# Position bias rows from a repeated table in memory, and another room for a low part

## The chip, the cores and the metric

The kernel runs on one core of one Trainium2 chip. TensorE (PE) multiplies matrices into PSUM; VectorE (DVE), ScalarE (ACT) and GpSimd (POOL) work on SBUF and PSUM; SyncE (SP) issues almost all transfers between the chip's memory (DRAM) and SBUF, which 16 DMA engines carry. The metric is the device time of one execution, in microseconds.

## The reference

One layer over 512 tokens of width 2048, in float32. Two mixers run in parallel on projections of the normalised input: a gated linear recurrence in 8 heads, and an attention of 8 heads in which an indexer picks 128 keys for each query and a position bias from a table of 32 buckets is added to the scores. Both are gated, projected, merged, projected out and normalised. What the change touches are the bias and the end of the recurrence:

```python
bias = jnp.moveaxis(bias_table[t5_bucket(top_idx - t_pos[None, :, None])], -1, 2)
logits = jnp.where(valid[:, :, None, :], logits + bias, -jnp.inf)
...
o = rmsnorm(o, gnorm_w).reshape(b_, s_, A_WIDTH)
return (o * jax.nn.silu(a_g.astype(F32))).astype(a_q.dtype)
```

The bias depends on key position minus query position alone. Over a block of 128 queries and the 256 keys that end with it, row p of the bias is the same row of 384 values, read from 127 - p on.

## The kernel before

Every float32 product is made of three products of a high and a low part (`split`, `mm3`): ScalarE rounds a tile to the high part, VectorE subtracts it for the low part. Weights come in blocks of 512 KB. `load` issues a block into one of two raw buffers (`wr`); a block is split when TensorE begins the block two ahead of it (`prep`, or `high_parts` with its `low_parts` one step later), and a raw buffer is free for the next load when the low part is made. `load_ahead` issues loads as buffers come free.

The order is written out by hand. `jobs` is a list of matmul jobs; each calls `pump()` every few matmuls. `pump()` issues free loads, calls `flush()` (which issues stores put off by two pumps, kept in `late`), and takes one step of each of six generators, its lanes: `hgrn`, `top`, `att`, `norm`, `misc`, `t5`. Every engine executes its own instructions in the order in which the program gives them; SP too has one such order.

`t5_gen` makes the bias. It multiplies the bias table by a one-hot matrix of buckets (two matmuls into 8 x 384), subtracts each head's first value, splits the result and stores both parts in memory (`t5_d`). Then, for two heads at a time, it loads 128 overlapping rows of 256 values with a step of one value between partitions (`bf`, a load for each part), multiplies both by a flipped identity (`flip`) so that the row order is reversed, copies the product out of PSUM and stores 128 x 256 values for each head in `bh_d`. Each pair of heads takes four steps of the lane. Before the attention, `att_bias(h)` loads `bh_d[h]`, and GpSimd adds it to the mask.

`hgrn_gen(p)` runs the recurrence for two heads at once (pairs 3, 2, 0, 1 in this order). It ends with `o` (in the room of `hf`), its squares (`hk`), their sums over a head (`hz`, matmuls with ones), and the gated output `hy`, of which high and low parts of two heads are stored in `ya_d` by four put-off stores. The rooms of these four parts are `hkd`, `hst`, `hq` and `hS`. For pairs 3, 2 and 0 the rooms of `hf`, `hk` and `hq` lie in the pool `norms`, which is given back before the attention; pair 0 uses those of pair 3. `hS` and `hkd` are one room for all pairs: the next pair's `hks` copy (L859) goes into the same one.

`ai_job(3)`, `ai_job(2)` and `af_aq(0)` are the matmul jobs that run while `t5_gen` and the first two recurrences do.

Of the kernel before, what the change touches and what calls it, by code (L numbers as in the profile page):

```python
# [44 lines left out]
F32 = mybir.dt.float32  # L45
FR = mybir.dt.float32r
AF = mybir.ActivationFunctionType
OP = mybir.AluOpType
# [4 lines left out]
T, D = 512, 2048  # L53
NK = D // 128
H, HD = 8, 128
# [13 lines left out]
def hybrid_block(ctx, tc, x, norm_w, w_in, lb_table, gnorm_a, q_norm_w, kv_norm_w, w_uq,  # L69
# [3 lines left out]
    V, A, G, PE, SP = nc.vector, nc.scalar, nc.gpsimd, nc.tensor, nc.sync  # L73
# [9 lines left out]
    dram = ctx.enter_context(tc.tile_pool(name="scratch", bufs=1, space=DRAM))  # L83
    ctx.enter_context(tc.manual_schedule())

    def bank(name):
        return sdp.tile([128, 512], F32, name=name, tag="sd")

    def split(hi, lo, src):
        A.activation(hi, src, AF.Copy)  # L90
        V.tensor_tensor(lo, src, hi.bitcast(F32), op=OP.subtract)  # L91
# [6 lines left out]
    def mm(ps, l, r, first, last):  # L98
        PE.matmul(ps, l, r, start=first, stop=last, skip_group_check=True)  # L99
# [13 lines left out]

    ya_d = dram.tile([2, H, 128, T], F32, name="ya_d")
    yb_d = dram.tile([2, H, 128, T], F32, name="yb_d")
    t5_d = dram.tile([2, H, 384], F32, name="t5_d")
    gate_d = dram.tile([48, 128, T], F32, name="gate_d")
    bh_d = dram.tile([H, 128, 256], F32, name="bh_d")
    m21_d = dram.tile([2, 128, 8, 256], F32, name="m21_d")
    ckv_d = dram.tile([2, 128, T], F32, name="ckv_d")  # L120
    cq_d = dram.tile([4, 128, T], F32, name="cq_d")
# [13 lines left out]
    R = SimpleNamespace(load=0.0)  # L135
# [82 lines left out]
    late = [[], []]  # L218
# [266 lines left out]
    def t5_gen():  # L485
        rb = R.i.tile([128, H], F32, name="rb")
        rbs = [R.i.tile([128, H], FR, name=f"rb{i}") for i in "hl"]
        oh = R.i.tile([128, 384], FR, name="oh")
        tl = R.i.tile([H, 384], F32, name="tl")
        ts = [R.i.tile([H, 384], FR, name=f"tl{i}", tag=f"sum{i}") for i in "hl"]  # L490
        flip = R.i.tile([128, 128], FR, name="flip")
        far = R.i.tile([H, 1], F32, name="far")
        G.memset(rb, 0.0)
        SP.dma_start(rb[0:32], rel_bias)
        raw = R.i.tile([128, 512], F32, name="nt", bufs=2)
        SP.dma_start(raw[:, 0:384], c_buckets)
        SP.dma_start(raw[:, 384:], c_flip)
        yield
        yield
        A.activation(oh, raw[:, 0:384], AF.Copy)  # L500
        A.activation(flip, raw[:, 384:], AF.Copy)
        split(*rbs, rb)
        yield
        ps = bank("t5")
        for i, r in enumerate(rbs):
            mm(ps[:H, :384], r, oh, i == 0, i == 1)
        V.tensor_copy(far, ps[:H, 0:1])
        V.tensor_scalar(tl, ps[:H, :384], far, None, op0=OP.subtract)
        A.activation(ts[0], tl, AF.Copy)
        yield  # L510
        V.tensor_tensor(ts[1], tl, ts[0].bitcast(F32), op=OP.subtract)
        for i in range(2):
            late[1].append(lambda i=i: SP.dma_start(t5_d[i], ts[i].bitcast(F32)))
        for _ in range(3):
            yield
        for h in range(0, H, 2):
            bf = R.i.tile([128, 2, 2, 256], FR, name="bf")
            for i in range(2):
                SP.dma_start(bf[:, i].bitcast(F32), bass.AP(tensor=t5_d.tensor, offset=t5_d.offset + (i * H + h) * 384,
                                                            ap=[[1, 128], [384, 2], [1, 256]]))  # L520
            for _ in range(3):
                yield
            ps = bank("t5")
            for i in range(2):
                mm(ps, flip, bf[:, i].rearrange("p h c -> p (h c)"), i == 0, i == 1)
            e = R.i.tile([128, 2, 256], F32, name="nt", bufs=2)
            V.tensor_copy(e, ps.rearrange("p (h c) -> p h c", h=2))
            late[1].append(lambda h=h, e=e: SP.dma_start(bh_d[h:h + 2].rearrange("h p c -> p h c"), e))
            yield

    def lb_gen():
# [182 lines left out]
    def place(p, shape, dtype, name, tag):  # L714
        if p == 1 or tag not in ("hf", "hk", "hq"):
            return R.h.tile(shape, dtype, name=name, tag=tag)
        return R.i.tile(shape, dtype, name=name, tag=f"{tag}{p or 3}")
# [60 lines left out]
    def aq_evac(p):  # L778
        def evac(c, ps):
            if c == 0:  # L780
                hg[p, "q"] = place(p, [128, 2, T], F32, "hq", "hq")
            q = hg[p, "q"][:, c, :]
            A.activation(q, ps, AF.Sigmoid)
            V.scalar_tensor_tensor(q, ps, 128 ** -0.5, q, op0=OP.mult, op1=OP.mult)
            if c == 1:
                lanes["hgrn"].append(hgrn_gen(p))
        return evac

    def hgrn_gen(p):
        f, k, q = (hg[p, n] for n in "fkq")  # L790
# [78 lines left out]
        for l in range(8):  # L869
# [10 lines left out]
            ps = bank("hl")  # L880
# [76 lines left out]
        for c in range(2):  # L957
            ps = bank("hz")
# [10 lines left out]
        yield  # L969
        R.load = 2.4  # L970
        for c in range(2):
            y = [place(p, [128, T], FR, f"hy{i}", (("hkd", "hst"), ("hq", "hS"))[i][c]) for i in range(2)]
            split(*y, sq[:, c])
            for i in range(2):
                late[1].append(lambda y=y[i], i=i, h=2 * p + c: SP.dma_start(ya_d[i, h], y.bitcast(F32)))
# [46 lines left out]

    def att_bias(h):
        bh = R.a.tile([128, 256], F32, name="bh")
        SP.dma_start(bh, bh_d[h])
        at_[h, "g"] = R.a.tile([128, T], F32, name="ag", bufs=2)
        SP.dma_start(at_[h, "g"], gate_d[8 + h])
        MB = R.a.tile([128, 4, 256], F32, name="MB")

        def add(b):  # L1030
            if b:
                e = MO[b] + (b + 1) * 128
                G.tensor_tensor(MB[:, b, :], R.M[:, e - 256:e], bh, op=OP.add)
            else:
                G.tensor_tensor(MB[:, 0, 128:], R.M[:, 0:128], bh[:, 128:], op=OP.add)

        return MB, add
# [71 lines left out]
    def att_gen(p):  # L1109
        def rest(n):  # L1110
            for _ in range(n + (p > 0)):
                yield

        while lanes["top"]:
            yield
        MB, add = att_bias(2 * p)
        for two in ((3, 2), (0, 1)):
            for b in two:
                add(b)
            yield  # L1120
        P = yield from att_scores(p, 0, MB)
        MB, add = att_bias(2 * p + 1)
        for two in ((3, 2), (0, 1)):
            for b in two:
                add(b)
            yield
        yield from rest(1)
        PT = att_turn(P)
        yield from rest(2)
        att_values(p, 0, PT)  # L1130
        P = yield from att_scores(p, 1, MB)
        yield from rest(3)
        PT = att_turn(P)
        yield from rest(2)
        att_values(p, 1, PT)
        yield
# [174 lines left out]
    def end_index():  # L1311
        lanes["misc"].extend(waiting)
        drain("misc")
        leave("idx")
        leave("raws")
        R.h = enter("hgrn", side="right")
        lanes["hgrn"].extend((hgrn_gen(3), hgrn_gen(2)))
        lanes["norm"].append(norm_gen(R.ckv, 2, c_kvw, R.ckh, R.ckl))
        lanes["t5"].append(t5_gen())
# [355 lines left out]
```

## Time and profile before

| what | us |
|---|---|
| median of three runs | 1349.22 (1348.98 to 1350.01) |
| the profiled execution's own time | 1349.49 |
| its span in the trace | 1347.7 |
| TensorE busy | 1336.3 |
| VectorE busy | 1073.1 |
| ScalarE busy | 686.8 |
| GpSimd busy | 26.5 |

In rows of the profile, L12 is line 12 of the kernel; `out<-in` are the tiles or tensors that an instruction writes and reads, with numbers left out of their names (`t<-bf,flip` is the bias product in the bank `t5`, `t_d` is `t5_d`). A row of the timeline starts with the start and the duration in us; in square brackets stands the idle time of the engine ahead of it and what ended it. SPq is SP issuing a transfer: the duration there is that of the issue, and several of a line are taken together. In a list of waits the numbers are total us, times, longest us. In the rows of transfers they are the count, the size of one and the median us from issue to landing. The granted clock of TensorE was 0.999.

### The profile page before, as it was taken

What the parts mean: (1) busy time and instruction counts of PE and PEld (TensorE: products, weight loads), DVE (VectorE), ACT (ScalarE), POOL (GpSimd) and SP (SyncE); (2) the same over time, 40 slices, a digit from 0 to 9 for tenths busy, and PEclk for the clock granted to TensorE, in tenths of its full rate; (3) what the DMA queues carried; (4) which work ended last, traced back from release to release, by engine and by line L of the source; (5) the groups of instructions that cost most, each with busy time, mean ns of one, the idle gap of its engine ahead of it and who ended that gap; (6) DMA issues with size and microseconds to landing.
All of it is one profiled execution on the core that took longest, in us unless ns stands there. A gap on an engine that the chain in (4) does not pass through costs nothing.

```text
span 1347.7 us, 26963 instructions
## 1 busy us (share of the span) xinstructions
PE 1336.3 (99%) x11018; PEld 1244.6 (92%) x11018; DVE 1073.1 (80%) x1750; ACT 686.8 (51%) x1108; POOL 26.5 (2%) x47
## 2 busy tenths in 40 slices
PE   9999999999999999999999999999999999999997
PEld 8888999999999999999999898888888888899996
DVE  7978889988798888886778877975656658899856
ACT  8555444545554444445765655656443433444444
POOL 0000000000000000000000000020101100000000
PEclk9999999999999999999999999999999999999999
DMA  6245345544444445446224533445855556653563
GB/s 226 71 120 153 95 142 171 157 141 143 140 145 120 128 141 157 142 141 208 71 79 132 169 99 91 125 135 182 279 182 185 185 183 211 211 157 119 170 228 141
DMA packets 145310, 204.80 MB, mean 152 GB/s; under 512 B 10601, under 2 KB 87074, under 8 KB 145058
## 3 DMA queue, kind: packets, MB, share of 16 engines
q1 hardware_dynamic: 144898, 202.82, 48.2%
q8 instruction: 86, 1.41, 0.4%
q14 instruction: 38, 0.31, 0.1%
q10 hardware_dynamic: 288, 0.26, 0.1%
HBM read 167.89 MB, written 35.15 MB: 151 GB/s over the span
## 4 chain that ended last, share of the span: by engine, by line
PE 97%; DMA 1%; ACT 1%; DVE 1%; issue 0%; SPq 0%; DVEq 0%; ACTq 0%
PE pp L94 15%; PE pp L96 15%; PE pp L95 15%; PE acc L94 14%; PE acc L96 14%; PE acc L95 14%; PE acc L99 2%; PE hl L99 1%; PE ho L99 1%; PE sc L94 1%; PE sc L95 1%; PE sc L96 1%; DMA ya_d<-hy 0%; DMA x<-in_x_dram 0%; PE hp L99 0%; PE pt L378 0%
## 5 line engine op out<-in xcount | busy, mean ns | idle before, releaser
L169 ACT ACTIVATE bh<-wr 128x768 fp32r<-128x768 f32 x128 | 108.2, 845 | 211.8 <-issue 88.7
L171 ACT ACTIVATE wh<-sv 128x512 fp32r<-128x512 f32 x256 | 152.8, 624 | 88.3 <-DVE sv L164 69.9
L94 PE MATMUL pp<-s,wh 128*128 128x256 f32 x624 | 172.3, 276 | 0.0
L95 PE MATMUL pp<-s,wh 128*128 128x256 f32 x624 | 172.3, 276 | 0.0
L96 PE MATMUL pp<-s,wl 128*128 128x256 f32 x624 | 172.3, 276 | 0.0
L173 DVE TENSOR_TENSOR wl<-sv,wh 128x1024 fp32r<-128x1024 f32 x128 | 156.5, 1222 | 5.8
L172 DVE TENSOR_TENSOR bl<-wr,bh 128x768 fp32r<-128x768 f32 x128 | 122.3, 955 | 40.4 <-ACT bh L169 40.3
L94 PE MATMUL acc<-xh,wh 128*128 128x512 f32 x304 | 120.9, 398 | 0.0
L91 DVE TENSOR_TENSOR wl<-wr,wh 128x1024 fp32r<-128x1024 f32 (+1 forms) x74 | 88.9, 1201 | 39.4 <-ACT wh L90 39.2
L96 PE MATMUL acc<-xh,wl 128*128 128x512 f32 x304 | 118.7, 390 | 0.0
L95 PE MATMUL acc<-xl,wh 128*128 128x512 f32 x304 | 118.4, 390 | 0.0
L95 PEld LDWEIGHTS pp<-s,wh 128*128 128x128 f32 x624 | 117.2, 188 | 0.0
L96 PEld LDWEIGHTS pp<-s,wl 128*128 128x128 f32 x624 | 117.1, 188 | 0.0
L94 PEld LDWEIGHTS pp<-s,wh 128*128 128x128 f32 x624 | 117.1, 188 | 0.0
L94 PE MATMUL pp<-xh,bh 128*128 128x256 f32 x416 | 114.9, 276 | 0.0
L96 PE MATMUL pp<-xh,bl 128*128 128x256 f32 x416 | 114.9, 276 | 0.0
L95 PE MATMUL pp<-xl,bh 128*128 128x256 f32 x416 | 114.9, 276 | 0.0
L90 ACT ACTIVATE wh<-wr 128x1024 fp32r<-128x1024 f32 (+1 forms) x74 | 76.6, 1035 | 70.4 <-PE acc L95 37.7
L94 PE MATMUL acc<-yh,wh 128*128 128x512 f32 x256 | 100.2, 391 | 0.0
L96 PE MATMUL acc<-yh,wl 128*128 128x512 f32 x256 | 99.8, 390 | 0.0
L95 PE MATMUL acc<-yl,wh 128*128 128x512 f32 x256 | 99.7, 390 | 0.0
L164 DVE TENSOR_TENSOR sv<-wr 128x512 f32<-128x512 f32 x128 | 87.9, 687 | 11.7 <-DMA wr<-in_w_in_dram 8.8
(406 smaller groups left out, 3724.2 us busy)
## 6 DMA issues: line engine op xcount, KB each, us to landing
wr<-in_w_in_dram SPq DMA_DIRECT2D x136, 512.0 KB, 3.8
wr<-in_w_out_dram SPq DMA_DIRECT2D x32, 512.0 KB, 3.7
mg<-gate_d SPq DMA_DIRECT2D x48, 256.0 KB, 3.4
gate_d<-c SPq DMA_DIRECT2D x44, 256.0 KB, 5.3
wr<-in_w_in_dram SPq DMA_DIRECT2D x36, 256.0 KB, 3.1
wr<-in_w_pa_dram SPq DMA_DIRECT2D x16, 512.0 KB, 4.2
wr<-in_w_pb_dram SPq DMA_DIRECT2D x16, 512.0 KB, 4.4
wr<-in_w_qidx_dram SPq DMA_DIRECT2D x8, 512.0 KB, 4.4
```

Of the source, the lines that this page charges most:

```text
L90: A.activation(hi, src, AF.Copy)
L91: V.tensor_tensor(lo, src, hi.bitcast(F32), op=OP.subtract)
L94: PE.matmul(ps, lh, rh, start=first, stop=False, skip_group_check=True)
L95: PE.matmul(ps, lh, rl, start=False, stop=False, skip_group_check=True)
L96: PE.matmul(ps, ll, rh, start=False, stop=last, skip_group_check=True)
L99: PE.matmul(ps, l, r, start=first, stop=last, skip_group_check=True)
L164: V.tensor_tensor(sv[:, 0:2, :], b[:, 1:3, :], b[:, 0:1, :].to_broadcast([128, 2, 256]), op=OP.add)
L169: A.activation(bh, b[:, 1:4, :], AF.Copy)
L171: A.activation(vh[:, i:i + 2, :], sv[:, i:i + 2, :], AF.Copy)
L172: V.tensor_tensor(bl, b[:, 1:4, :], bh.bitcast(F32), op=OP.subtract)
L173: V.tensor_tensor(vl, sv, vh.bitcast(F32), op=OP.subtract)
```

## The change

The table `tl` (8 heads x 384 values, float32) is stored once, unsplit, in `t5_d`. For two heads at a time a transfer within memory copies each head's row 128 times into `bh_d`, which is now 128 x 384 for each head; the four transfers are issued in four steps of the lane in a row. `att_bias` reads row p of head h from element 127 - p on, by a step of 383 elements between partitions. The matmuls with `flip`, the split of the table, the loads of `bf` and the copies out of PSUM are gone. Apart from that, the low part of the second head of `hy` takes the room of `hf` in place of that of `hS`.

```diff
-    t5_d = dram.tile([2, H, 384], F32, name="t5_d")
+    t5_d = dram.tile([H, 384], F32, name="t5_d")
-    bh_d = dram.tile([H, 128, 256], F32, name="bh_d")
+    bh_d = dram.tile([H, 128, 384], F32, name="bh_d")
...
-        ts = [R.i.tile([H, 384], FR, name=f"tl{i}", tag=f"sum{i}") for i in "hl"]
-        flip = R.i.tile([128, 128], FR, name="flip")
...
-        raw = R.i.tile([128, 512], F32, name="nt", bufs=2)
-        SP.dma_start(raw[:, 0:384], c_buckets)
-        SP.dma_start(raw[:, 384:], c_flip)
+        raw = R.i.tile([128, 384], F32, name="nt", bufs=2)
+        SP.dma_start(raw, c_buckets)
...
-        A.activation(ts[0], tl, AF.Copy)
-        yield
-        V.tensor_tensor(ts[1], tl, ts[0].bitcast(F32), op=OP.subtract)
-        for i in range(2):
-            late[1].append(lambda i=i: SP.dma_start(t5_d[i], ts[i].bitcast(F32)))
-        for _ in range(3):
+        late[1].append(lambda: SP.dma_start(t5_d, tl))
+        for _ in range(4):
             yield
         for h in range(0, H, 2):
-            bf = R.i.tile([128, 2, 2, 256], FR, name="bf")
-            for i in range(2):
-                SP.dma_start(bf[:, i].bitcast(F32), bass.AP(tensor=t5_d.tensor, offset=t5_d.offset + (i * H + h) * 384,
-                                                            ap=[[1, 128], [384, 2], [1, 256]]))
-            for _ in range(3):
-                yield
-            ps = bank("t5")
-            for i in range(2):
-                mm(ps, flip, bf[:, i].rearrange("p h c -> p (h c)"), i == 0, i == 1)
-            e = R.i.tile([128, 2, 256], F32, name="nt", bufs=2)
-            V.tensor_copy(e, ps.rearrange("p (h c) -> p h c", h=2))
-            late[1].append(lambda h=h, e=e: SP.dma_start(bh_d[h:h + 2].rearrange("h p c -> p h c"), e))
+            SP.dma_start(bh_d[h:h + 2], bass.AP(tensor=t5_d.tensor, offset=t5_d.offset + h * 384,
+                                                ap=[[384, 2], [0, 128], [1, 384]]))
             yield
...
-            y = [place(p, [128, T], FR, f"hy{i}", (("hkd", "hst"), ("hq", "hS"))[i][c]) for i in range(2)]
+            y = [place(p, [128, T], FR, f"hy{i}", (("hkd", "hst"), ("hq", "hf"))[i][c]) for i in range(2)]
...
-        SP.dma_start(bh, bh_d[h])
+        SP.dma_start(bh, bass.AP(tensor=bh_d.tensor, offset=bh_d.offset + h * 128 * 384 + 127,
+                                 ap=[[383, 128], [1, 256]]))
```

More of the change, by code (lines that the diff above doesn't have):

```diff
@@ L494, in t5_gen @@
         SP.dma_start(rb[0:32], rel_bias)
-        raw = R.i.tile([128, 512], F32, name="nt", bufs=2)
-        SP.dma_start(raw[:, 0:384], c_buckets)
-        SP.dma_start(raw[:, 384:], c_flip)
+        raw = R.i.tile([128, 384], F32, name="nt", bufs=2)
+        SP.dma_start(raw, c_buckets)
         yield
         yield
-        A.activation(oh, raw[:, 0:384], AF.Copy)
-        A.activation(flip, raw[:, 384:], AF.Copy)
+        A.activation(oh, raw, AF.Copy)
         split(*rbs, rb)
```

## The prediction

> **What bounds the kernel now.** I read the page first, then who waited for whom on TensorE, then the chain, and then the DMA queue and ScalarE in order of time around the work that the change touches.
>
> ```profile
> PE 1336.3 (99%) x11018; PEld 1244.6 (92%) x11018; DVE 1073.1 (80%) x1750; ACT 686.8 (51%) x1108; POOL 26.5 (2%) x47
> PE 97%; DMA 1%; ACT 1%; DVE 1%; issue 0%; SPq 0%; DVEq 0%; ACTq 0%
> PE acc L335 <- POOL ones_r L305: 1.4, 1, 1.4
> ...
> PE hl L99 <- ACT hks L859: 0.4, 1, 0.4
> PE acc L95 <- issue: 0.3, 1, 0.3
> ```
>
> TensorE is busy for 1336.3 us of a span of 1347.7, and 97% of the chain is its own. Its waits are five rows (the first and the last two are shown) of 3.5 us in all. So time is won here only by taking instructions off TensorE, or those 0.4 us, and anything that makes TensorE wait is paid in full.
>
> **The removed work.** The flipped products are eight matmuls in four pairs; the first and the last of the four on the chain are these.
>
> ```profile
> 713.43 0.47 PE t L99 x2
> ...
> 754.67 0.47 PE t L99 x2
> ```
>
> Four pairs at 0.47 make 1.9 us. What goes with them (four copies out of PSUM and a subtraction on VectorE, two casts on ScalarE) lies beside a busy TensorE, since no row of its waits names them: nothing. If that cover were gone, it would still be a gain.
>
> **The other room.** The low part of the second head now lies where that pair's `o` was, and not in `hS`. What waited for `hS` stands on the chain.
>
> ```profile
> 802.52 6.12 DMA ya_d<-hy
> 808.72 1.07 ACT hks L859
> ```
>
> ScalarE's copy at 808.72 waited for a store of pair 2, and TensorE waited 0.4 us behind it: -0.4. The new room has later users too: pair 3's becomes pair 0's `hf`, and the rooms of pairs 2 and 0 become the attention's tiles. The nearest is pair 0's, at the last stores before the attention's `aq`:
>
> ```profile
> 858.55 2.35 SPq L975 DMA_DIRECT2D ya_d<-hy  x4
> ...
> 869.35 0.60 ACT L987 ACTIVATE aq<-acc 128x512 fp32r<-128x512 f32 x1 [0.91 <-PE acc L96]
> ```
>
> The last is issued by 860.9 and such a store lands in 4.8 (row below), at 865.7, ahead of 869.35: nothing. Uncovered, it would cost at most those 4.8 us.
>
> **The loads of the bias.** Eight loads of 128 rows of 1 KB stay eight, at addresses shifted by a row.
>
> ```profile
> ya_d<-hy SPq DMA_DIRECT2D x16, 256.0 KB, 4.8
> bf<-t_d SPq DMA_DIRECT2D x8, 256.0 KB, 4.3
> bh_d<-nt SPq DMA_DIRECT2D x4, 256.0 KB, 5.0
> bh<-bh_d SPq DMA_DIRECT2D x8, 128.0 KB, 4.1
> ```
>
> Their landing is bounded by 4.1 and, doubled, 8.2 us. Behind a load queue GpSimd's additions and VectorE's maxima; none of TensorE's five waits names these. Nothing, with at most 4 us at the first head if the cover fails.
>
> **The copies in memory.** This part decides. Eight loads of `bf` and four stores go; four copies come, memory to memory, each of 2 heads x 128 rows x 384 elements, 1,536 B to a row and 393,216 B to a copy. SP does not wait for TensorE, so where they come to stand is read from its queue.
>
> ```profile
> 696.57 0.40 SPq L513 DMA_DIRECT2D t_d<-tlh  x1
> 697.02 0.30 SPq L513 DMA_DIRECT2D t_d<-tll  x1
> 702.94 0.40 SPq L147 DMA_DIRECT2D wr<-in_w_in_dram  x1
> 703.43 0.97 SPq L519 DMA_DIRECT2D bf<-t_d  x2
> 708.75 0.37 SPq L147 DMA_DIRECT2D wr<-in_w_in_dram  x1
> 709.17 0.50 SPq L919 DMA_DIRECT2D hg<-gate_d  x1
> 718.15 0.37 SPq L147 DMA_DIRECT2D wr<-in_w_in_dram  x1
> ```
>
> The generator takes seven steps to the first transfer before and after, so copy 1 stands at 703.4. Before, the next pair came four steps later; now the copies stand in four steps in a row. Between two weight loads lie two steps, and a copy waits for nothing: copies 1 and 2 are issued at about 703.5 and 704, ahead of the weight load of 708.75 (call it W2), copies 3 and 4 at about 709.7 and 710.2, ahead of that of 718.15 (W3).
>
> What a copy costs behind it hangs on how many DMA engines carry it. The stretch from 696.3 to 702.9 (40 slices of 0.165 us), in which the two small stores follow a weight load, shows this:
>
> ```profile
> GB/s 0 0 0 0 0 68 124 87 137 106 180 304 366 391 391 379 379 236 146 34 0 0 99 0 0 0 0 0 0 0 0 0 0 0 0 0 0 0 0 0
> DMA packets 561, 0.57 MB, mean 86 GB/s; under 512 B 32, under 2 KB 560, under 8 KB 560
> ...
> wr<-in_w_in_dram SPq DMA_DIRECT2D x1, 512.0 KB
> t_d<-tlh SPq DMA_DIRECT2D x1, 12.0 KB
> t_d<-tll SPq DMA_DIRECT2D x1, 12.0 KB
> ```
>
> 561 packets are 512 rows of weights, 16 rows of 1,536 B, one instruction fetch, and 32 tiny ones. A transfer that counts 128 partitions first and two that count 8 rows first would leave 16 + 8 + 8 = 32 completions: I read these as one for each engine used, and the engines as dealt along the outermost count. The copies count 2 heads outermost. So they would run on two of the 16 engines, each with one head: 196,608 B. The trace holds no transfer of size with a short outermost count, so this price is bounded. Below: all 16 engines at 385 GB/s (the mean of the load's four best slices above) carry 393,216 B in 1.0 us, which delays nothing. Above: two engines at the mean of the stretch around it,
>
> ```profile
> q1 hardware_dynamic: 13363, 14.09, 40.9%
> ```
>
> 14.09 MB in 40.9% of 16 engines over 120 us (660 to 780): 17.9 GB/s for an engine, 11.0 us a copy. At the best slices' 24.1 GB/s for an engine it is 8.2 us. I take two engines, by the completions, and 8.2, since rows of 1.5 KB stand nearer to the best slices' rows of 1 KB than to a mean with single words in it.
>
> The Trainium skill ("DMA: Bandwidth & Descriptors", "Why a DMA increments its semaphore by 16 and not by 1") says that a transfer uses the largest number of engines up to 16 that divides the outermost counts of both its sides. The trace agrees as far as the 16 + 8 + 8 go. With that page's 27 GiB/s for an engine a copy would take 6.8 us (an estimate), and the sum below would be 5.6 us lower.
>
> The queue is one, so the weights' share on those two engines stands behind the copies. A load occupies the engines until about 3.3 us after its issue (traffic above ends in slice 20, at 699.6; it was issued some 0.3 ahead of the 696.57), 1.4 of them at full rate. From the load of 702.94: free at 706.2; copies 1 and 2 to 722.6; W2 to 724.0; `hg` to 725.4; copies 3 and 4 to 741.8; W3 to 743.2, landed by 743.6. Here is who wants them:
>
> ```profile
> 719.21 1.06 ACT L208 ACTIVATE wh<-wr 128x1024 fp32r<-128x1024 f32 x1
> ...
> 725.27 1.06 ACT L208 ACTIVATE wh<-wr 128x1024 fp32r<-128x1024 f32 x1 [0.99 <-PE acc L96]
> 726.36 1.28 ACT L961 ACT_TABLE_LOAD   x1
> 728.46 1.27 ACT L961 ACTIVATE hk<-hz,cols 128x512 f32<-128x512 f32 x2 [0.82 <-PE hz L99]
> 729.75 1.28 ACT L962 ACT_TABLE_LOAD   x1
> 731.04 1.06 ACT L962 ACTIVATE hk<-hk 128x1024 f32<-128x1024 f32 x1
> 732.00 1.07 ACT L743 ACTIVATE hv<-acc 128x512 f32<-128x512 f32 x2
> 732.96 1.06 ACT L208 ACTIVATE wh<-wr 128x1024 fp32r<-128x1024 f32 x1
> ...
> 736.22 0.63 ACT L90 ACTIVATE hy<-hk 128x512 fp32r<-128x512 f32 x1 [0.69 <-DVE hk L968]
> ```
>
> ```profile
> 737.96 0.39 PE L96 MATMUL acc<-xh,wl 128*128 128x512 f32 x1
> ...
> 745.34 0.40 PE L96 MATMUL acc<-xh,wl 128*128 128x512 f32 x1
> ```
>
> ```profile
> 732.19 1.22 DVE L211 TENSOR_TENSOR wl<-wr,wh 128x1024 fp32r<-128x1024 f32 x1
> ```
>
> With two raw buffers, W2 is split at 719.21 and W3 at 725.27; weights are split two blocks ahead, and W3's block starts with the third matmul, its first use of a low part, at 737.96. Now W2 makes ScalarE wait 5 us from 719.21; what that costs TensorE is swallowed by the next. W3 lands at 743.6: split to 744.7, low part to 745.9 instead of 737.96: 7.9 us of TensorE. Behind the waiting split stand ScalarE's table loads, logarithms, exponentials and copies of `hv` (1.28 + 1.27 + 1.28 + 1.06 + 1.07, to 750.7), the next split (751.7), two `hy` (753.0), and VectorE's last `hy` and low part (0.7 + 1.2: 754.9). That low part is the one of the next block, used at 745.34: the shift is now 9.6. The pairs of products ahead of it are within the stall and give nothing; the last pair and the room give 0.47 + 0.4 behind it. **The sum: +8.7 us.** On the profiled execution's 1349.49 that is 1358.2; it was 0.27 above the median of 1349.22, so I predict **1357.9** for the median. At 11.0 us a copy W3 lands 11.2 later: 1369.1. Below, 16 engines: -1.9 - 0.4, 1346.9.
>
> **The rivals.** No change here means within 0.2%, 2.7 us, about what a measurement of this kernel can tell.
> 1. *The rows, and not the heads, are dealt to the engines.* A copy is then 256 rows over 16 engines, 1.0 us, and the slack of W3 (landed at 718.15 + 3.8, split at 725.27) takes four of them: 1346.9, not slower. It decides from about 2 us a copy down. For it: all loads of size in the trace fill 16 engines. Against: 32 completions and not 48. Chance 0.20.
> 2. *The cover holds.* If copies 3 and 4 come to stand behind W3, it lands by 726, and only the load after it is late, at 743.6 against a split at 732.96; the two blocks ahead then absorb all but some 2.5 us, which the removed products pay: 1349.5. Against: nothing keeps SP from issuing them earlier. Chance 0.08.
> 3. *A row from memory to memory takes twice as long* (a read and a write at the same memory): 16.4 us a copy, 32.8 later, 1390.7. The stores' 4.8 us against the loads' 4.3 for the same 256 KB speak against double. Chance 0.05.
> 4. *Copies on 16 engines, and the freed engines or the moved tiles give more than the products.* TensorE's other waits are 3.5 - 0.4 us, so at most 3.1 more: 1343.8. They lie elsewhere in the code, which speaks against it. Chance 0.05.
>
> **How the numbers follow.** The forecast, a stall at W3, has 0.62. Slower: 0.62 + 0.05 = 0.67. Within 0.2%: the second rival's 0.08 and 0.13 of the first's, whose 2.3 us lie just inside: 0.21. Faster: the rest of the first, 0.07, and the fourth: 0.12. The forecast's own range is 1355 to 1369: its low end is the sum without the catch-up after W3 (7.9, less the two pairs behind it and the 0.4: +6.6), its high end 11.0 us a copy; with the first rival taken in it is 1346.4 to 1369, which leaves out the third, the fourth and the tails.
>
> **What would show it.** Right: the copies issued on SP at about 703.5, 704, 709.7 and 710.2, landing after 10 us and more, later ones later; a wait of ScalarE's split for weights of some 5 us near 719 and 15 or more near 726; a hole in TensorE near 738; no product on `flip`; no wait of `hks` for `ya_d`. The prediction is wrong if the copies land in about 5 us, if the weight loads behind them keep 3.8, or if the hole is elsewhere.

## The result and the profile after

The changed kernel takes 1360.37 us (median; 1359.5 to 1361.63) against 1349.28 beside it: a ratio of 1.0082, 95% interval 1.0069 to 1.0095. It is 11.1 us slower; 8.7 were forecast. The profiled execution's span grew from 1347.7 to 1359.8 us, by 12.1. That execution took 1361.63 us, 1.3 above the median of its kernel, so a sum read from its trace comes out about 1 us above the 11.1.

From the page of the changed kernel, engines and chain:

```profile
PE 1339.5 (99%) x11010; PEld 1245.6 (92%) x11010; DVE 1070.5 (79%) x1745; ACT 686.5 (50%) x1106; POOL 27.4 (2%) x47
...
PE 92%; DMA 3%; DVE 2%; ACT 1%; issue 1%; SPq 0%; DVEq 0%; ACTq 0%
```

TensorE has eight products less, and yet 3.2 us more busy time; its share of the chain fell from 97% to 92%. Who waited for whom on TensorE says where the rest went (total us, times, longest us):

```profile
PE acc L94 <- ACT wh L208: 4.7, 1, 4.7
PE hl L99 <- DVE hqs L809: 3.2, 1, 3.2
...
PE hz L99 <- DVE hzl L91: 1.2, 1, 1.2
```

Three new holes, 9.1 us. The wait of `hl` for `hks` behind the store is gone. On SP, the queue of transfers in order of time (start and duration in us):

```profile
703.25 0.37 SPq L147 DMA_DIRECT2D wr<-in_w_in_dram  x1
703.67 3.91 SPq L509 DMA_DIRECT2D bh_d<-t_d  x2
709.06 6.26 SPq L147 DMA_DIRECT2D wr<-in_w_in_dram  x1
715.37 1.91 SPq L901 DMA_DIRECT2D hg<-gate_d  x1
717.33 8.46 SPq L509 DMA_DIRECT2D bh_d<-t_d  x2
725.91 28.32 SPq L147 DMA_DIRECT2D wr<-in_w_in_dram  x4
```

The copies (L509) stand in the order that was expected, two ahead of the weight load W2 (709.06) and two ahead of W3 (725.91). The second two come later than expected, at 717.33 and 718.3 and not at 709.7 and 710.2, since SP was taken for 6.26 us by issuing W2 and for 1.91 by `hg`. What moved in the stretch from 704 to 742, in 40 slices of 0.95 us (busy share of the 16 DMA engines in tenths, then GB/s):

```profile
DMA  5951111111113897921111111111121379794111
GB/s 70 320 198 50 50 50 50 50 50 52 49 50 82 224 350 160 361 108 50 47 51 50 50 50 50 52 50 50 50 67 50 66 193 357 156 322 172 50 49 47
```

Whenever only copies move, it is at 50 GB/s, an eighth of the 385 of a weight load, and the digit is 1: two engines of 16, at 25 GB/s each, 7.9 us for 196,608 B. (The trace has no landing time of the copies themselves; the 7.9 us are worked out from this rate.) The chain, in order of time, shows what this does to the weights and how it reaches TensorE:

```profile
709.06 14.90 DMA wr<-in_w_in_dram
...
725.91 16.36 DMA wr<-in_w_in_dram
742.36 1.06 ACT wh L208
...
752.57 1.22 DVE wl L211
753.79 1.15 DVE hqs L809
754.98 1.05 PE hl L99 x64
```

W2 is there at 724.0 (forecast: through the engines at 724.0) and W3 at 742.4 (forecast: 743.6); loads that landed in 3.8 us take 14.9 and 16.4. ScalarE, whose splits stood at 719.21 and 725.27, waits for both:

```profile
723.99 1.06 ACT L208 ACTIVATE wh<-wr 128x1024 fp32r<-128x1024 f32 x1 [4.73 <-DMA wr<-in_w_in_dram]
...
742.36 1.06 ACT L208 ACTIVATE wh<-wr 128x1024 fp32r<-128x1024 f32 x1 [15.16 <-DMA wr<-in_w_in_dram]
```

Behind the two larger holes the granted clock was low. Of the stretches from 743.5 to 746.9 and from 754.98 to 760.6 (length, busy us and count by engine, granted clock, share of the DMA engines, GB/s):

```profile
743.50:746.90 3.40, 3.21 (x7) 2.11 (x8) 1.17 (x1) 3.37 (x4) 0.00 (x0) 0.52 0.30 63
...
754.98:760.60 5.62, 5.62 (x75) 4.63 (x76) 5.45 (x13) 2.47 (x4) 0.00 (x0) 0.50 0.95 289
```

In these stretches a matmul of 128x512 starts every 0.43 us, and at full clock every 0.23. So TensorE did in 9.0 us what takes some 5, and most of the added busy time comes from here.

### The profile page after: what moved, and what is told of

It is laid out like the page before. It is cut to its first block, busy times and chain, and to the rows that moved or that the text cites. A ratio compares the mean times of both kernels' runs of the same rounds, so it can differ in the third digit from the quotient of the medians.

```text
span 1359.8 us, 26916 instructions
## 1 busy us (share of the span) xinstructions
PE 1339.5 (99%) x11010; PEld 1245.6 (92%) x11010; DVE 1070.5 (79%) x1745; ACT 686.5 (50%) x1106; POOL 27.4 (2%) x47
## 4 chain that ended last, share of the span: by engine, by line
PE 92%; DMA 3%; DVE 2%; ACT 1%; issue 1%; SPq 0%; DVEq 0%; ACTq 0%
PE pp L96 15%; PE pp L95 15%; PE pp L94 15%; PE acc L94 13%; PE acc L95 13%; PE acc L96 13%; DMA wr<-in_w_in_dram 2%; PE acc L99 2%; PE hl L99 1%; PE ho L99 1%; PE sc L94 1%; PE sc L95 1%; PE sc L96 1%; DMA fr<-in_w_in_dram 0%; PE pt L378 0%
```

## The experiments

**Rows outermost.** Only the order in which a copy counts:

```diff
-            SP.dma_start(bh_d[h:h + 2], bass.AP(tensor=t5_d.tensor, offset=t5_d.offset + h * 384,
-                                                ap=[[384, 2], [0, 128], [1, 384]]))
+            SP.dma_start(bh_d[h:h + 2].rearrange("h p c -> p h c"),
+                         bass.AP(tensor=t5_d.tensor, offset=t5_d.offset + h * 384,
+                                 ap=[[0, 128], [384, 2], [1, 384]]))
```

> The changed kernel with one edit: each of the four copies counts its 128 rows outermost and the two heads inside, the same bytes at the same places of the queue. Theory (a transfer is dealt to the engines along its outermost count, and two engines were the fault): 16 engines carry a copy, about 1.0 us of each, no wait of the weight splits at 719 and 726, no hole in TensorE at 738, granted clock 1.00 there; the four product pairs and the 0.4 us are all that is left of the change: 1349.3 - 2.3 = 1347.0, against 1360.4 for the changed kernel. Rival (a copy from memory to memory is slow by itself, or the bias loads at shifted addresses cost): 1355 to 1361, and the splits still wait 5 and 15 us.

Measured: 1347.1 us (1346.32 to 1348.82), ratio 0.9981 (0.9973 to 0.9990). Its transfers (count, KB each, median us to landing):

```profile
bh_d<-t_d SPq DMA_DIRECT2D x4, 384.0 KB, 5.5
...
bh<-bh_d SPq DMA_DIRECT2D x8, 128.0 KB, 4.3
```

The same bytes between the same places land in 5.5 us, ScalarE's splits stand at 718.84 and 725.00 again, and TensorE has no wait behind them:

```profile
718.84 1.06 ACT L208 ACTIVATE wh<-wr 128x1024 fp32r<-128x1024 f32 x1
725.00 1.06 ACT L208 ACTIVATE wh<-wr 128x1024 fp32r<-128x1024 f32 x1 [1.00 <-PE acc L96]
```

So copying within memory is not slow as such, the bias loads at shifted addresses cost TensorE nothing (4.3 us to landing against 4.1), and the order of two counts is worth 13 us. This version beats both kernels.

**The room alone.** The kernel before with one word changed:

```diff
-(("hkd", "hst"), ("hq", "hS"))[i][c]
+(("hkd", "hst"), ("hq", "hf"))[i][c]
```

> The kernel before with the other room for the second head's low part and nothing else. Theory (TensorE waited 0.4 us behind the copy into hS, and nothing waits for the new room): 1349.3 - 0.4 = 1348.9, no wait of the hks copy for a store of hy. Rival (the new room makes a later tile wait, and takes part in the loss): 1350 or more, with a wait for ya_d at another line.

Measured: 1349.28 us against 1349.54, ratio 0.9996 (0.9988 to 1.0005). From its timeline:

```profile
805.30 1.04 ACT L859 ACTIVATE hks<-hk 128x1024 f32<-128x1024 f32 x1
```

The copy into `hks`, at 808.72 before behind the store, waits for nothing, and no later tile waits for `ya_d`. The size, 0.3 us, is below what the interval tells from no change.

**Four heads and eight heads to a copy.** Heads stay outermost; 4 stands for two copies, 8 for one:

```diff
-        for h in range(0, H, 2):
-            SP.dma_start(bh_d[h:h + 2], ... ap=[[384, 2], [0, 128], [1, 384]]))
+        for h in range(0, H, 4):
+            SP.dma_start(bh_d[h:h + 4], ... ap=[[384, 4], [0, 128], [1, 384]]))
```

> The changed kernel with two copies of four heads each in place of four copies of two, heads still outermost. Theory (as many engines as heads, 196,608 B to an engine for each copy at about 8.2 us): four engines are taken for 16.4 us in place of two for 32.8. Both copies stand ahead of the weight load of 709, which lands as late as in the changed kernel (its split waits some 5 us and TensorE some 1.2 us for the squares), but the load of 718 lands at about 726 and its split hardly waits: no hole at 738, no half clock: 1347.0 + 1.2 = 1348.2. Rival (the two lowest engines carry every such copy, whatever the count): as slow as the changed kernel, 1360.

> The changed kernel with one copy of all eight heads, heads outermost. Theory: eight engines are taken once for 8.2 us; the weight load of 709 lands at about 716, ahead of its split at 719, and nothing waits: 1347.0. Rival (the two lowest engines carry it): 1360; rival (all bytes take the queue's time however they are dealt): no different from four heads.

Measured: four heads 1349.06 us (ratio 0.9994, 0.9985 to 1.0003), eight heads 1347.32 us (0.9982, 0.9972 to 0.9991). The traffic with four heads, from 703 to 726 in slices of 0.575 us:

```profile
GB/s 0 18 137 267 374 203 104 99 99 104 96 104 99 99 104 96 104 99 99 104 96 132 114 229 366 347 132 148 252 377 388 390 322 180 100 105 100 98 94 61
```

and with eight, from 703 to 714 in slices of 0.275 us:

```profile
GB/s 0 34 104 89 186 328 395 369 354 222 190 201 190 212 190 212 184 218 184 272 162 190 162 201 181 209 199 229 225 359 387 402 387 385 408 410 402 404 278 194
```

100 and 200 GB/s follow the 50 of two heads: as many engines as heads, each at 25 GB/s. With four heads the first split of the two is late as in the changed kernel and the second hardly:

```profile
723.61 1.06 ACT L208 ACTIVATE wh<-wr 128x1024 fp32r<-128x1024 f32 x1 [4.59 <-DMA wr<-in_w_in_dram]
726.73 1.04 ACT L208 ACTIVATE wh<-wr 128x1024 fp32r<-128x1024 f32 x1
```

TensorE's one new wait there is the 1.1 us for the squares, and the clock is 1.00 throughout. The time is 2.0 us above that with rows outermost (1.4 between the two profiled spans); 1.2 were worked out.

**The copies further apart.** One copy every four steps, as the pairs of loads were before:

```diff
                                                 ap=[[384, 2], [0, 128], [1, 384]]))
-            yield
+            for _ in range(4):
+                yield
```

> The changed kernel with the four copies four steps of the lane apart, as the pairs of loads were before; heads stay outermost, two engines carry each. Theory (the backlog of four copies ahead of two weight loads is the fault, and a single one of 8.2 us is covered by the blocks split ahead): the first copy is done at 714.4, the weight load behind it lands at about 716 against a split at 719; each later one the same: 1347.0, at most one split that waits 1 or 2 us. Rival (any copy on two engines delays a weight load by its whole length and TensorE by much of it): 4 x 3 us or more, 1355 to 1360.

Measured: 1346.95 us, ratio 0.9982 (0.9973 to 0.9991). Two splits wait, and nothing comes of it:

```profile
746.18 1.06 ACT L208 ACTIVATE wh<-wr 128x1024 fp32r<-128x1024 f32 x1 [2.08 <-DMA wr<-in_w_in_dram]
750.18 1.06 ACT L208 ACTIVATE wh<-wr 128x1024 fp32r<-128x1024 f32 x1 [1.45 <-DMA wr<-in_w_in_dram]
```

With two engines for each copy there is no loss, as long as the copies do not stand in a row. The loss of 13 us takes both: the short outermost count, and four copies ahead of two weight loads. (Two copies of four heads ahead of one load cost 2.0.)

**The copies alone.** The kernel before, with the four copies added into a tensor that nobody reads, in four steps in a row:

```diff
+    rep_d = dram.tile([H, 128, 384], F32, name="rep_d")
...
+        def copy(h):
+            SP.dma_start(rep_d[h:h + 2], bass.AP(tensor=t5_d.tensor, offset=t5_d.offset + h * 384,
+                                                 ap=[[384, 2], [0, 128], [1, 384]]))
...
+            if h == 0:
+                copy(0)
-            for _ in range(3):
+            for j in (2, 4, 6):
                 yield
+                if h == 0:
+                    copy(j)
```

> The kernel before, with all its products and loads, and in addition the four copies by heads, in four steps in a row from the first loads of bf on, into a tensor of their own that nobody reads. Theory (the copies' queue on two engines is the whole loss, whatever else is removed): TensorE's holes and the half clock as in the changed kernel; the product pairs ahead of the late weights lie in the holes, the two behind cost their 0.9 us, and the 0.4 us behind the store return: 1360.4 + 1.3 = 1361.7, with the loads of bf queued behind the copies perhaps 1 to 3 more. Rival (the loss is in what the bias loads or the moved tiles do): 1349 to 1352.

Measured: 1366.11 us, ratio 1.0123 (1.0109 to 1.0137), 16.7 us slower. The copies alone make the loss, and more of it than was expected, since another transfer is then behind them:

```profile
743.74 1.38 PE L99 MATMUL t<-bf,flip 128*128 128x512 f32 x2 [12.70 <-DMA bf<-t_d]
```

The second pair of `bf` loads is issued at 734.18, behind the copies and W3, where it was issued at 718.62 before, and the flipped product stands in TensorE's order ahead of the block that waits for W3. So TensorE has one hole of 12.7 us in place of the two of 4.7 and 3.2.

**The holes filled.** The changed kernel with 20 and 18 products of ones in TensorE's two larger holes, into a bank that nobody reads:

```diff
+    def fill(n):
+        warm = bank("warm")
+        for _ in range(n):
+            PE.matmul(warm, ones_r, xh[0][:, 0, :], start=True, stop=True, skip_group_check=True)
...
+            if (p, l) == (2, 1):
+                fill(18)
             scores(l, ps[:, at[1]:], qs2[1], kf)
...
-        feat_job(w_in, 1024 + p * 256, 2, NK, 4, x_rhs, af_evac(p), late_lows=True)
+        feat_job(w_in, 1024 + p * 256, 2, NK, 4, x_rhs, af_evac(p), late_lows=True,
+                 after={0: lambda: fill(20)} if p == 0 else None)
```

> The changed kernel with work put into TensorE's two largest holes: 20 products of 128x512 with ones (0.23 us each, into a bank that nobody reads) ahead of the second block of the first forget product, and 18 between the two score products of pair 2's first level. They leave the output as it is. In the changed kernel the granted clock is 0.50 for 3.4 us from 743.6 and for 6.8 us from 753.9, right behind the two holes. Theory A (TensorE's own idling brought the half clock): no stretch at 0.50 there, and although TensorE does 38 products more, the time falls by what the second half-speed stretch costs, some 2.5 to 3 us: 1357.5. Theory B (the half clock comes from something else, or its time is hidden by the late weights): the stretches stay, and the time is 1360.4 or more.

Measured: 1359.65 us, ratio 1.0073 (1.0060 to 1.0087). The stretches at half clock are gone (length, busy us and count by engine, granted clock, DMA):

```profile
744.00:748.00 4.00, 3.85 (x17) 3.23 (x18) 0.27 (x2) 3.96 (x6) 0.00 (x0) 1.00 0.44 131
...
756.00:760.00 4.00, 4.00 (x20) 3.29 (x19) 3.93 (x8) 2.03 (x3) 0.00 (x0) 1.00 1.01 351
```

That TensorE's idling brings the half clock is shown. The time fell by 0.7 us where 2.9 were expected, so the two were timed again, on one chip:

> The changed kernel as it is, on one chip with the next run, since the filled holes were 0.7 us faster where 2.5 to 3 were expected and the two were timed on different chips. Both theories: 1360.4, with the granted clock at 0.50 behind the holes.

> The filled holes again, beside the changed kernel on the same chip. Theory A (what the half clock costs behind the second hole is real time): 1.9 to 2.5 us below the changed kernel, the lead that TensorE's rows had from 764 to 794 after the landing of the late weights is taken off. Theory B (the lead is lost later, or was an accident of one profile): within 0.7 us of it.

Measured: the changed kernel 1359.85 us (ratio 1.0080, 1.0067 to 1.0094), the filled one 1360.01 (1.0081, 1.0067 to 1.0095): no difference. In this pair of profiles the changed kernel's first stretch at half clock was 6.8 us long and its second 3.4, the reverse of its first profile. Both profiles of the filled kernel have a wait, at 822.4 and at 823.4, that no engine explains and that the changed kernel doesn't have (first profile, then the repeat):

```profile
PE acc L94 <- issue: 0.8, 1, 0.8
...
PE acc L94 <- issue: 1.3, 1, 1.3
```

Held against the changed kernel matmul by matmul, the filled one gains 2.5 us in the first pair of profiles and 1.5 in the repeat, from the second score products of pair 2 to the end of the next block. It has lost 0.7 and 0.6 of it by 772, and another 0.9 and 1.2 by 850, behind that wait. What is left, a lead of 0.9 and a lag of 0.3, is near what the medians say (0.7 faster, 0.2 slower). So the half clock is real, its cause is shown, and behind the holes it costs 1.5 to 2.5 us. Why the filled kernel gives that back further on stays open, and with it the price in the median, between nothing and 2.5 us.

## Why the prediction was right

- **The bound.** Right: TensorE set the time, and its new waits are the loss.
- **The removed products and the room, -2.3.** Right. Without the fault of the copies the change is 2.4 us faster (rows outermost: 1347.1 against 1349.54; 2.3 were worked out). The room's wait is gone, its 0.4 us are not resolved.
- **The bias loads, nothing.** Right: 4.3 us to landing in the kernel with rows outermost, and no wait of TensorE.
- **Where the copies stand.** Right for the order in SP's queue, and wrong in that a copy waits for nothing on SP: the fourth copy's issue alone took 7.5 us, and W3 was issued at 725.91 and not at 718.15. It changed nothing, as W3 had to pass the same two engines, and these were never idle (no slice of the traffic from 707 to 742 is below 47 GB/s).
- **Two engines, 8.2 us a copy.** Right, and now seen: 50, 100, 200 GB/s for 2, 4 and 8 heads, 7.9 us a copy. The rule of the Trainium skill ("DMA: Bandwidth & Descriptors", "Why a DMA increments its semaphore by 16 and not by 1") that the prediction names agrees with this. The 27 GiB/s (29 GB/s) that the same page of the Trainium skill gives for an engine ("Specifications") are not reached here; 25 GB/s are.
- **W3 at 743.6, TensorE held 7.9 us.** Right in its way, 1.1 us too long. W3 came at 742.4, which is what the same sum gives with 7.9 us a copy. The third matmul of its block started at 744.73 instead of 737.96: 6.8. The 1.2 us that TensorE waited for the squares behind W2 are swallowed by this, as forecast. (The 3.3 us for which a load occupies the engines are 3.45, as that load was issued at 696.15; this moves nothing.)
- **The catch-up, to 9.6.** This step failed: it takes VectorE's low part for the last thing ahead of the next block, and its term was too small. The low part was made by 753.8 (forecast 754.9). But ahead of that block stand the scores of pair 2, and they wait for `hqs`, which VectorE makes behind that low part. They ran from 754.98 to 756.0, and the block's third matmul started at 756.99 and not at 754.9: 11.65 us late (756.99 - 745.34). The half clock, which the prediction didn't have at all, then adds about 1.8: the next scores start 13.42 late (763.92 - 750.50). (Some 0.7 more of it lies within the 11.65.) 13.42, less the 0.47 and 0.4 that come back, is 12.55; the spans differ by 12.1.
- **The number.** That 8.7 came as near to 11.1 as it did is in part luck: the hold at W3 was 1.1 us too long, the catch-up 3.2 too short (4.9 and not 1.7), and the half clock was missing.
- **The rivals.** Dealing by rows fell: it is what happens if the rows are outermost. The cover that holds fell for this order and is what the spread copies show. Rows at double time fell: 25 GB/s for an engine. Freed time elsewhere: nothing of it is seen.

## What to carry to other kernels

Look at the outermost count of a transfer and at what stands behind it in its queue: a broadcast written heads first ran on as many engines as heads, and four such copies cost 13 us, while the same bytes rows first, all heads at once, or a few steps apart cost nothing. In a profile this looks like a low and very even rate (50 GB/s in slice after slice, a 1 among the tenths) and a transfer behind it that lands late. Removing TensorE's work in a kernel that TensorE bounds paid about the 2.3 us that were worked out, once nothing new stood in front of the weights (2.4, 2.2 and 2.5 us in the three runs without a loss).

## What was not expected of the hardware

- **Half clock behind short holes.** Behind a hole of 4.7 us the granted clock was 0.5 for 3.4 us, and again from just before the end of one of 3.2 us, for 6.8. In the repeat it was so for 6.8 us from within the hole of 4.7, and for 3.4 behind one of 2.4. Holes of 1.1 and 1.2 us had no such stretch behind them. The Trainium skill ("TensorE: Matmul & The Clock Gate", "Part 1: The HAM clock gate") says that the clock drops to half after an idle window of about 3.4 us; the first hole agrees, the shorter ones show that the window need not be without any work. In the clock records of the traces every stretch at half clock is a multiple of 3.41 us long (17.07 with the copies alone), and so is the full clock between two of them. Read as a grid of 3.41 us, the clock fell behind the five cells in which TensorE was busy for 0.2 to 1.3 us. A full clock stayed full behind every cell with 1.7 us or more, in all eleven traces, and a halved one came back only behind a cell full of work. So where the grid falls on a hole decides how long the clock is halved, and that differs from execution to execution. Five falls show this reading; no run was made to test it.
- **SP is held by its own transfers.** In a row, issuing a copy on two engines took up to 7.5 us, against 0.6 with rows outermost and 0.6 to 0.7 when the copies on two engines stood four steps apart:

```profile
L509 SPq DMA_DIRECT2D bh_d<-t_d x4: 696/2056/7462, 703.7 to 718.3; - x4
```

(ns, shortest, median, longest, of the changed kernel.) What stands behind on SP is late even before it reaches an engine: issuing W2 took 6.26 us, against 0.37 before.
